# Local attention with TensorE's order written out: projections of the next head group and gates in small steps between scores, transposes and values

## The chip, the cores and the metric

The kernel runs on one core of a Trainium2 chip. A time is what the device reports for one execution, in microseconds (us). A profile is one further execution, recorded by the hardware profiler. Five engines work side by side, each through its own list of instructions in order: TensorE (PE in the profile, its weight loads PEld), VectorE (DVE), ScalarE (ACT), GpSimd (POOL) and SyncE (SP), which here only starts transfers. Semaphores hold an instruction until what it needs from another engine is done.

## The reference

One layer of an encoder on x of 1024 positions by 1024 features, with a cross-attention memory of 256 rows: RMSNorm; one input projection into attention q, k, v, a Mamba-2 branch and two gates; both branches merged by the gates; then cross-attention and an MLP. The change lies in the attention branch. There, 16 query heads of 64 features share 4 key/value heads, four to one; each block of 128 queries sees its own block of keys and those beside it (256 keys at the two edges of the sequence, 384 elsewhere):

```python
s = jnp.einsum('bnqgrd,bnkgd->bngrqk', qb, kw) * (d ** -0.5) + bias      # bias: ALiBi and the band
m = jnp.maximum(jnp.max(s, axis=-1, keepdims=True), sink_f)
p = jnp.exp(s - m)
denom = jnp.sum(p, axis=-1, keepdims=True) + jnp.exp(sink_f - m)
o = jnp.einsum('bngrqk,bnkgd->bnqgrd', p / denom, vw)
...
merged = sigmoid(gate_a) * (attn @ w_attn_branch) + sigmoid(gate_b) * (ssd @ w_ssd_branch)
```

## The kernel before

The phases follow one another: norms and transposes, the Mamba branch (`ssd`, whose TensorE order is already written by hand), attention (`attn_phase`, L584), merge and cross-attention (`merge_cross_phase`, L719), the MLP. Products are kept exact by splitting each operand into a high and a low part: `mm3` (L77) issues three matmuls per block of the inner dimension, hi·hi (L81), hi·lo (L85), lo·hi (L86). A projection of 128 features for all 1024 positions is 48 such matmuls of 512 columns, accumulated in one two-bank PSUM buffer of the pool `pg` (2 buffers). Its weights come by `wload`: a transfer started by SP into raw (2 buffers), a copy by ACT to whi (L66), a subtraction by POOL to wlo (L67).

Attention runs over four head groups kv, one key/value head with its four query heads each. Ahead of a group's blocks stand, in the program text, the K projection (kps; every second group, giving two heads kh and kl), for the first group the V projection (vp), four bias tables, and two Q projections (qps, four heads q). ACT and DVE copy each projection out of PSUM into halves that are 64 rows by 1024. Behind the blocks of a group stands one gate of ATT_GATES (gate_block, L302: a projection gps, two tanh on ACT, a store). A group has eight query blocks. For one block:

- `scores(qb)`: for each of four heads two matmuls sps (L667, L668) of 384 columns (256 at the edges), then one DVE reduction that adds the bias, writes the tile t4 (named t_… in the order) and its minimum nm (L669). On the four minima DVE then computes nm and es (L671, L672). ACT takes exp of es (L673) and of the four heads (L675), with their sums den; DVE adds and inverts den (L677, L678); POOL scales the four heads (L680).
- `values(qb)`: for each of three key blocks (two at the edges) four transposes into pt (L690), an ACT copy ph (L693) and a DVE remainder pl (L694); then two matmuls per key block into op (L699 with ph, L700 with pl). ACT copies both halves of op to oa and ob (L703, L704), POOL adds them (L705), SP stores the result to memory (d_at).

pt, sps and op share the pool `pp`, four PSUM buffers that are given out in turn. t4 has three buffers, ph and pl four, oa two, ob one. The scores of a block are issued two blocks ahead of its values.

What sets the order around the change: in `attn_phase` nothing is pinned, so a scheduler at build time orders the instructions of every engine by its own estimate of when each could start, across groups. On TensorE it thus mixes the projections of the next group and the gates between the matmuls of the blocks. The merge (L719) begins with the two END_GATES, 14 and 15, each with its first matmul kept in program order (L737, L738); then it loads the attention output back (at, 8 tiles, split by ACT at L733 and DVE at L734) and the Mamba output (yk), and multiplies them with weights into mps.

Of the kernel before, what the change touches and what calls it, by code (L numbers as in the profile page):

```python
# [11 lines left out]
ALU = mybir.AluOpType  # L12
# [17 lines left out]
ATT_GATES = ((10,), (11,), (12,), (13,))  # L30
# [553 lines left out]
def attn_phase(kx, ins, dr):  # L584
    nc, tc = kx.nc, kx.tc
    V, A, G, PE = nc.vector, nc.scalar, nc.gpsimd, nc.tensor
    with tc.tile_pool(name="p2", bufs=1) as ap:
# [30 lines left out]
        kd = {}  # L618
        for kv in range(4):
            if kv % 2 == 0:  # L620
                w = wload(kx, ins["wk"][kv // 2])
                ps = kx.pg.tile([P, S], F32, tag="g", name="kps")
                for h in range(2):
                    gemm_fm(kx, ps[:, h * 512:(h + 1) * 512], w, kx.hT[h])
# [9 lines left out]
            if kv == 0:  # L634
                v_part()
            qs, bias = [], []
            for i in range(4):
                bt = ap.tile([P, 384], F32, tag="bias", bufs=5, name="bias")
                A.activation(bt, rel, AF.Copy, scale=SLOPES[4 * kv + i])
                bias.append(bt)  # L640
            for i in range(2):
                w = wload(kx, ins["wq"][2 * kv + i])
                ps = kx.pg.tile([P, S], F32, tag="g", name="qps")
                for h in range(2):
                    gemm_fm(kx, ps[:, h * 512:(h + 1) * 512], w, kx.hT[h])
                for s in range(2):
# [4 lines left out]
                    qs.append((q, own))  # L651
            kh, kl = kd[kv]
            def scores(qb):
                kb0, kb1 = max(qb - 1, 0), min(qb + 2, NT)
                nb = kb1 - kb0
                n = nb * P
                bo = (kb0 - qb + 1) * P
                ql = slice(qb * P, (qb + 1) * P)
                keys = slice(kb0 * P, kb1 * P)
                t4 = ap.tile([P, 4, 384], F32, tag="t4", bufs=3, name="t4")  # L660
                nm = ap.tile([P, 4], F32, tag="nm", bufs=2, name="nm")
                den = ap.tile([P, 4], F32, tag="den", bufs=2, name="den")
                es = ap.tile([P, 4], F32, tag="es", bufs=2, name="es")
                for i in range(4):
                    q, own = qs[i]
                    sp_ = kx.pp.tile([P, 512], F32, tag="p", name="sps")
# [681 lines left out]
```

## Time and profile before

| | |
|---|---|
| runs shown | 2495.89 us median of 3 (2494.34 to 2497.92) |
| the profiled execution | 2500.91 us, its span 2499.1 us |
| granted clock, mean | 0.989 of full speed |
| TensorE busy | 2409.9 us, 96% |
| DVE, ACT, POOL busy | 1357.4, 1072.5, 1054.1 us |
| first score matmul to last values matmul | 1014.0 to 1292.0 us |
| four head groups, by their first score matmul | 69, 80, 70 and 59 us |

Times in the profile are microseconds from the start of the span. A row of a timeline gives start, duration, engine, line, operation, tile written <- tiles read, count, and in brackets the idle time before it with what ended it. Several equal instructions in a row are one row with their count, and the duration is then from the first start to the last end. A matmul row's duration overlaps the next one's, since TensorE works as a pipeline; the cost of a matmul is the distance to the next start.

### The profile page before, as it was taken

To read this page: it belongs to the slowest core of one execution; us is meant where nothing else is said; L and a number is where in the kernel's file an instruction comes from. 1 tells how busy PE (TensorE), PEld (TensorE's weight loads), DVE (VectorE), ACT (ScalarE), POOL (GpSimd) and SP (SyncE) were. 2 spreads that over 40 slices of the span, in tenths; PEclk is the share of its full clock that TensorE was granted. 3 is DMA by queue.
4 is the path that set the end of the run, shared out by engine and by line. 5 is a ranking of instruction groups with operands and counts; after the bars stand their busy time and mean duration, and the time that the engine had idled before them with its cause. 6 is when DMAs were issued, how large, how long until landed. Compare 5 with 4: busy or idle time off the path is not lost.

```text
span 2499.1 us, 32531 instructions
## 1 busy us (share of the span) xinstructions
PE 2409.9 (96%) x12156; PEld 1998.4 (80%) x12156; DVE 1357.4 (54%) x2048; ACT 1072.5 (43%) x2214; POOL 1054.1 (42%) x905
## 2 busy tenths in 40 slices
PE   7899999999999999999999999999999998999998
PEld 6688887878878788777778878888978876788887
DVE  5747566575665753555554352235775555454534
ACT  5436355463544544676773242235543323221211
POOL 4234526354363633444444444134685544231210
PEclk9999999999999999999999999999999998999999
DMA  6223223232322422111135453411443334442211
GB/s 224 79 66 119 68 85 109 61 122 63 103 89 74 125 64 73 43 41 47 49 120 175 148 203 121 160 68 58 136 166 114 114 127 143 173 135 85 90 62 68
DMA packets 154926, 260.47 MB, mean 104 GB/s; under 512 B 11792, under 2 KB 86672, under 8 KB 154768
## 3 DMA queue, kind: packets, MB, share of 16 engines
q1 hardware_dynamic: 83872, 219.58, 25.7%
q10 hardware_dynamic: 70896, 38.81, 5.5%
q8 instruction: 96, 1.57, 0.3%
q14 instruction: 62, 0.51, 0.1%
HBM read 210.90 MB, written 47.45 MB: 103 GB/s over the span
## 4 chain that ended last, share of the span: by engine, by line
PE 64%; DVE 13%; POOL 8%; ACT 7%; issue 6%; DMA 2%; SPq 0%; ACTq 0%; POOLq 0%; DVEq 0%
PE pb L1108 5%; PE dps L85 5%; PE dps L86 5%; PE dps L81 5%; PE mps L85 3%; PE mps L86 3%; PE mps L81 3%; PE zp L85 2%; PE zp L81 2%; PE zp L86 2%; PE pc L1108 2%; PE st L462 2%; DVE cx L350 2%; POOL prev L477 2%; POOL cb_t L476 1%
## 5 line engine op out<-in xcount | busy, mean ns | idle before, releaser
L67 POOL TENSOR_TENSOR wlo<-raw,whi 128x1024 fp32r<-128x1024 f32 x142 | 346.8, 2443 | 595.4 <-ACT whi L66 559.8
L66 ACT ACTIVATE whi<-raw 128x1024 fp32r<-128x1024 f32 x144 | 152.0, 1056 | 253.5 <-PE mps L85 115.1
L81 PE MATMUL cps<-kt,whi 128*128 128x512 f32 x512 | 217.9, 426 | 8.6 <-DVE cx L350 8.6
L86 PE MATMUL cps<-kt,wlo 128*128 128x512 f32 x512 | 201.6, 394 | 0.0
L85 PE MATMUL cps<-kt,whi 128*128 128x512 f32 x512 | 201.4, 393 | 0.0
L1074 POOL TENSOR_TENSOR wop<-w,wop 128x512 fp32r<-128x512 f32 x64 | 92.9, 1458 | 94.0 <-ACT wop L1073 94.0
L81 PEld LDWEIGHTS cps<-kt,whi 128*128 128x128 f32 x512 | 97.5, 190 | 35.0 <-issue 16.3
L85 PEld LDWEIGHTS cps<-kt,whi 128*128 128x128 f32 x512 | 97.6, 191 | 26.3 <-issue 7.3
L86 PEld LDWEIGHTS cps<-kt,wlo 128*128 128x128 f32 x512 | 97.3, 190 | 21.0
L120 POOL TENSOR_TENSOR rr<-rv,mhalf 128x1 f32<-128x1 f32 (+1 forms) x50 | 38.6, 772 | 170.1 <-DVE rv L118 167.5
L81 PE MATMUL gps<-kt,whi 128*128 128x512 f32 x256 | 108.8, 425 | 0.0
L496 ACT ACTIVATE ef<-rows,ebias 128x128 f32<-128x128 f32 x256 | 83.2, 391 | 53.3 <-PE cb L511 50.1
L680 POOL TENSOR_SCALAR t<-t,den 128x384 f32<-128x384 f32 (+1 forms) x128 | 69.1, 559 | 82.0 <-DVE den L678 62.9
L85 PE MATMUL mps<-yk,whi 128*128 128x512 f32 x256 | 100.2, 391 | 1.5 <-DVE yk L734 1.4
L86 PE MATMUL gps<-kt,wlo 128*128 128x512 f32 x256 | 101.5, 396 | 0.0
L85 PE MATMUL gps<-kt,whi 128*128 128x512 f32 x256 | 100.9, 394 | 0.0
L86 PE MATMUL mps<-yk,wlo 128*128 128x512 f32 x256 | 99.8, 390 | 0.3 <-POOL wlo L67 0.3
L81 PE MATMUL mps<-yk,whi 128*128 128x512 f32 x256 | 99.9, 390 | 0.0
L85 PE MATMUL dps<-kt 128*128 128x512 f32 x256 | 99.7, 389 | 0.0
L81 PE MATMUL dps<-kt 128*128 128x512 f32 x256 | 99.7, 389 | 0.0
L85 PE MATMUL dps<-wd,u 128*128 128x512 f32 x256 | 99.7, 389 | 0.0
L86 PE MATMUL dps<-wd,u 128*128 128x512 f32 x256 | 99.7, 389 | 0.0
(369 smaller groups left out, 7144.8 us busy)
## 6 DMA issues: line engine op xcount, KB each, us to landing
rows<-d_cs ACTq DMA_DIRECT2D x128, 256.0 KB, 3.8
raw<-in_wssd_dram SPq DMA_DIRECT2D x48, 512.0 KB, 3.3
raw<-in_wup_dram SPq DMA_DIRECT2D x40, 512.0 KB, 3.8
raw<-in_wsb_dram SPq DMA_DIRECT2D x32, 512.0 KB, 3.2
d_u<-c SPq DMA_DIRECT2D x64, 256.0 KB, 3.0
uraw<-d_u SPq DMA_DIRECT2D x32, 512.0 KB, 4.0
raw<-in_wdn_dram SPq DMA_DIRECT2D x28, 512.0 KB, 4.3
x<-in_x_dram SPq DMA_DIRECT2D x16, 512.0 KB, 7.4
```

What stands on the lines that cost most here:

```text
L66: nc.scalar.activation(hi, raw, AF.Copy)
L67: (eng or nc.gpsimd).tensor_tensor(lo, raw, hi.bitcast(F32), ALU.subtract)
L81: i = mm(out, l[0], r[0], start=first, stop=False)
L85: mm(out, l[0], r[1], start=False, stop=False)
L86: mm(out, l[1], r[0], start=False, stop=last)
L350: V.scalar_tensor_tensor(acc[:, :S - o], ps[:, o:], cw(k), acc[:, :S - o], ALU.mult, ALU.add)
L462: PE.matmul(st[:, lo:hi], q.btok[:, c], xs.rearrange("p d h q -> p (d h q)")[:, lo:hi], start=True, stop=True)
L477: G.tensor_tensor(prev[:, c - 1, 1], prev[:, c - 1, 1], t, ALU.add)
L496: A.activation(ef[:, h], rows[:, 0, h], AF.Exp, bias=kx.ebias[:, b, j, 0, o:o + 1])
L680: G.tensor_scalar(t4[:, i, :n], t4[:, i, :n], den[:, i:i + 1], 1.0, ALU.mult, ALU.mult)
L1074: self.kx.nc.gpsimd.tensor_tensor(t[:, 1], src, t[:, 0].bitcast(F32), ALU.subtract)
L1108: self.kx.nc.tensor.matmul(ps, w[:, i, ks], act[:, k, j], start=start and k == 0 and m == 0, stop=k == 3 and m == 2, skip_group_check=True)
```

## The change

Only `attn_phase` and ATT_GATES change. TensorE's order in the phase is now the order of the program text (`manual_schedule` for PE); ACT, DVE, POOL and SP are still ordered by the scheduler. The K and Q projections and the gates 10 to 13 become jobs of a `Stream`. A job is cut into 16 chunks of three matmuls, and its weights are loaded when the job ahead of it begins. The text takes each block apart into units: the three (at the edges two) sets of four transposes of the block itself (`flips`), and the four scores of the block two ahead; then the values of the block itself. `deal` spreads a given number of chunks evenly in front of these units, and the table `counts` gives the number for each of the 32 blocks. Of 14 jobs' 224 chunks 48 run ahead of the first score (as in before: a K and two Q projections with V between them), 7 in the first two scores, the rest by the table. Jobs with flag 1 are held: their matmuls run, but the copies out of PSUM are issued only with `release`, at block 5 of a group, together with the next group's bias tables. These are the last Q job of each next group and the K job of groups 2 and 3. No chunk of the END_GATES is dealt: they stay in `merge_cross_phase`.

```diff
-ATT_GATES = ((10,), (11,), (12,), (13,))
+ATT_GATES = (10, 11, 12, 13)
...
-    with tc.tile_pool(name="p2", bufs=1) as ap:
+    with tc.tile_pool(name="p2", bufs=1) as ap, tc.manual_schedule(engines={mybir.EngineType.PE}):
...
+        def k_job(kv):
+            def load():
+                return wload(kx, ins["wk"][kv // 2])
+            def run(w):
+                ps = psum_g(kx, "kps")
+                yield from fm_chunks(kx, ps, w)
...
-            t4s = {0: scores(0), 1: scores(1)}
-            for qb in range(NT):
-                if qb + 2 < NT:
-                    t4s[qb + 2] = scores(qb + 2)
-                values(qb, t4s[qb])
-            for m in ATT_GATES[kv]:
-                gate_block(kx, ins, dr, m)
+        class Stream:
...
+            def take(self, n):
+                for _ in range(n):
+                    if self.cur is None:
+                        if not self.jobs:
+                            return
+                        (_, run), hold = self.jobs.pop(0)
+                        w, self.w = self.w, self.jobs[0][0][0]() if self.jobs else None
+                        self.cur, self.left, self.hold = run(w), 16, hold
+                    next(self.cur)
+                    self.left -= 1
+                    if not self.left:
+                        if self.hold:
+                            self.held.append(self.cur)
+                        else:
+                            self.end(self.cur)
+                        self.cur = None
...
+        s = Stream([(k_job(0), 0), (q_job(0, 0), 0), (q_job(0, 1), 0), (q_job(1, 0), 0), (q_job(1, 1), 1),
+                    (gate_job(ATT_GATES[0]), 0), (q_job(2, 0), 0), (q_job(2, 1), 1), (k_job(2), 1),
+                    (gate_job(ATT_GATES[1]), 0), (q_job(3, 0), 0), (q_job(3, 1), 1)]
+                   + [(gate_job(m), 0) for m in ATT_GATES[2:]])
+        s.take(16)
+        v_part()
+        s.take(32)
+        bias_of(0)
...
+        def deal(units, n):
+            for i, unit in enumerate(units):
+                s.take((i + 1) * n // len(units) - i * n // len(units))
+                unit()
+        for b in range(2):
+            t4s[b], units = scores(0, b)
+            deal(units, 3 + b)
+        counts = ((6, 6, 6, 5, 5, 5, 2, 1), (9, 9, 9, 9, 9, 8, 3, 3), (7, 7, 7, 7, 7, 7, 3, 3),
+                  (4, 4, 3, 3, 3, 3, 3, 3))
+        for b in range(4 * NT):
+            kv, qb = divmod(b, NT)
+            pts = []
+            units = flips(qb, t4s.pop(b), pts)
+            if b + 2 < 4 * NT:
+                t4s[b + 2], more = scores((b + 2) // NT, (b + 2) % NT)
+                units += more
+            deal(units, counts[kv][qb])
+            if qb == 5 and kv < 3:
+                s.release()
+                bias_of(kv + 1)
+            values(kv, qb, pts)
+        s.take(16)
```

On TensorE, in a block of the last head group with three chunks: before had values, transposes and scores of several blocks mixed one by one, with single gate matmuls (gps) between them. Here t_11799 is block 26's tile, and the words in brackets are the engines whose semaphores the instruction waits for:

```order
L690 MATMUL pt<-ident,t_11799 128x128 [waits DVE_49,Pool_49]
L690 MATMUL pt<-ident,t_11799 128x128 [waits Pool_49] x2
L699 MATMUL op<-ph,vhl 128x512 [waits Activation_49]
L690 MATMUL pt<-ident,t_11799 128x128 [waits Pool_49]
L690 MATMUL pt<-ident,t_11799 128x128 [waits DVE_49]
L690 MATMUL pt<-ident,t_11799 128x128 x3
L85 MATMUL gps<-kt,whi 128x512
L700 MATMUL op<-pl,vhl 128x512 [waits DVE_49]
```

On this engine, in after, with t_11846 as block 27's tile, the transposes stand together, then the scores with three-matmul chunks between them, then the values:

```order
L711 MATMUL pt<-ident,t_11846 128x128 [waits DVE_49]
L711 MATMUL pt<-ident,t_11846 128x128 x3
L687 MATMUL sps<-kh,q 128x384 [waits PE_49,Activation_49]
L688 MATMUL sps<-kl,q 128x384
L81 MATMUL gps<-kt,whi 128x512
L85 MATMUL gps<-kt,whi 128x512
L86 MATMUL gps<-kt,wlo 128x512
L687 MATMUL sps<-kh,q 128x384 [waits DVE_49]
```

The first score matmul waits for ACT, which must have copied the op of the block before out of the same PSUM buffer; the next waits for DVE, which must have read a pt.

On ACT, also in the last group, before had the two copies of op ahead of the next exponentials. Here t_11799 and t_11861 are the tiles of blocks 26 and 27:

```order
L673 ACTIVATE es<-es 128x4
L675 ACTIVATE t_11799,den<-t_11799,nm 128x384 x4
L693 ACTIVATE ph<-pt 128x512 x3
L703 ACTIVATE oa<-op 64x512
L704 ACTIVATE ob<-op 64x512
L673 ACTIVATE es<-es 128x4
L675 ACTIVATE t_11861,den<-t_11861,nm 128x384 x4
```

Now, with t_11931 and t_12019 as the tiles of blocks 28 and 29:

```order
L697 ACTIVATE t_11931,den<-t_11931,nm 128x384
L695 ACTIVATE es<-es 128x4
L697 ACTIVATE t_11931,den<-t_11931,nm 128x384 x3
L729 ACTIVATE oa<-op 64x512
L730 ACTIVATE ob<-op 64x512
L714 ACTIVATE ph<-pt 128x512 x3
L729 ACTIVATE oa<-op 64x512
L695 ACTIVATE es<-es 128x4
L697 ACTIVATE t_12019,den<-t_12019,nm 128x384 x4
L730 ACTIVATE ob<-op 64x512
```

Both copies, or ob alone, now stand behind the exponentials of the block two ahead, and the copies ph of the next block behind these.

On DVE, before reduced the four scores of a block with one pl among them (block 27's tile t_11861):

```order
L694 TENSOR_TENSOR pl<-pt,ph 128x512
L669 ISA t_11861,nm<-sps,bias 128x384
L669 ISA nm 128x1
L669 ISA t_11861,nm<-sps,bias 128x384
L669 ISA nm 128x1
L669 ISA t_11861,nm<-sps,bias 128x384
L669 ISA nm 128x1
L677 TENSOR_TENSOR den<-den,es 128x4
L669 ISA t_11861,nm<-sps,bias 128x384
L669 ISA nm 128x1
L678 RECIPROCAL den<-den 128x4
L694 TENSOR_TENSOR pl<-pt,ph 128x512
```

Now the first reduction of a block (29, t_12019) stands ahead of the three pl of block 27, and its other three behind them:

```order
L699 TENSOR_TENSOR den<-den,es 128x4
L700 RECIPROCAL den<-den 128x4
L689 ISA t_12019,nm<-sps,bias 128x384
L689 ISA nm 128x1
L715 TENSOR_TENSOR pl<-pt,ph 128x512 x3
L689 ISA t_12019,nm<-sps,bias 128x384
L689 ISA nm 128x1
L689 ISA t_12019,nm<-sps,bias 128x384
```

At the end of the phase, before had 52 of the 96 matmuls of END_GATES ahead of the last values matmul and 44 behind it, ahead of the first mps; now all 96 stand behind it. The order of mps and of everything later, and of all ahead of the first score, is the same in both.

162 lines of the change are left out of this document (92 added, 70 removed).

## The prediction

> **What bounds the kernel now.** I read the page's first and fourth parts first, then the row of the attention stretch by windows, then a timeline of one block inside it.
>
> ```profile
> PE 2409.9 (96%) x12156; PEld 1998.4 (80%) x12156; DVE 1357.4 (54%) x2048; ACT 1072.5 (43%) x2214; POOL 1054.1 (42%) x905
> PE 64%; DVE 13%; POOL 8%; ACT 7%; issue 6%; DMA 2%; SPq 0%; ACTq 0%; POOLq 0%; DVEq 0%
> ```
>
> TensorE is busy for 96% of the span and carries 64% of the chain that ended last, so a change of order can only win back its waits. The change touches one stretch, from the first score matmul (1014.0) to the last values matmul (1292.0), and the seam behind it. Windows, for all instructions; the columns are the window, its length, then busy time and count of PE, PEld, DVE, ACT and POOL, the granted clock and the DMA share:
>
> ```profile
> 1014.00:1292.00 278.00, 273.85 (x1366) 213.62 (x1365) 169.69 (x490) 199.83 (x489) 137.25 (x171) 1.00 0.15 45
> 1233.00:1292.00 59.00, 57.66 (x293) 44.48 (x292) 39.18 (x120) 44.68 (x116) 31.00 (x41) 1.00 0.13 41
> ```
>
> "Busy" overstates the work there, since matmuls overlap in the pipeline; the distance between starts is what each costs. Timeline rows of PE, at places where nothing waits (start, duration):
>
> ```profile
> 1036.21 0.34 PE L667 MATMUL sps<-kh,q 128*128 128x384 f32 x1
> 1036.38 0.34 PE L668 MATMUL sps<-kl,q 128*128 128x384 f32 x1
> ...
> 1051.46 1.47 PE L690 MATMUL pt<-ident,t 128*128 128x128 f32 x12
> 1052.69 0.48 PE L86 MATMUL qps<-kt,wlo 128*128 128x512 f32 x1
> ...
> 1074.08 0.40 PE L81 MATMUL qps<-kt,whi 128*128 128x512 f32 x1
> ...
> 1082.71 0.40 PE L86 MATMUL qps<-kt,wlo 128*128 128x512 f32 x1
> 1082.94 0.28 PE L667 MATMUL sps<-kh,q 128*128 128x256 f32 x1
> 1083.06 0.28 PE L668 MATMUL sps<-kl,q 128*128 128x256 f32 x1
> ```
>
> A projection matmul costs 0.227 us (38 intervals from 1074.08 to 1082.71), a transpose 0.10 to 0.12 (twelve between 1051.46 and 1052.69 or, by their 1.47, to the last end; I take 0.11), a score matmul 0.175 over 384 keys and 0.12 over 256; a values matmul has the projection's 512 columns, so 0.227. By the code and the order of before, the stretch holds 580 projection matmuls (11 jobs of 48, and 52 of the end gates), 352 transposes, 192 and 64 score matmuls, and 176 of values: 131.7 + 38.7 + 33.6 + 7.7 + 40.0 = 251.7 us. Of the 278.0, 26.3 is waiting. That is all that a better order could win here.
>
> **The change, part by part.** First the move of the end gates. After puts all 96 matmuls behind the last values; before had 44 there. The stretch loses 52 × 0.227 = 11.8 us of work (floor 239.9) and the time behind it gains the same, which is nothing by itself. But in before the merge starved at the seam. PE and ACT rows there, and the row of the mps matmuls alone by windows (length, PE busy and count, PEld, clock):
>
> ```profile
> 1292.04 0.59 ACT L703 ACTIVATE oa<-op 64x512 f32<-64x512 f32 x1 [0.34 <-PE op L700]
> ...
> 1302.09 1.34 ACT L733 ACTIVATE at<-at 128x512 fp32r<-128x512 f32 x2 [7.89 <-DMA at<-d_at]
> ...
> 1305.90 3.23 ACT L733 ACTIVATE at<-at 128x512 fp32r<-128x512 f32 x6 [0.41 <-ACT gt L312]
> ```
> ```profile
> 1301.60 0.39 PE L86 MATMUL gps<-kt,wlo 128*128 128x512 f32 x1
> 1302.77 0.50 PE L81 MATMUL mps<-at,whi 128*128 128x512 f32 x1 [0.78 <-ACT at L733]
> ...
> 1306.58 0.50 PE L81 MATMUL mps<-at,whi 128*128 128x512 f32 x1 [1.64 <-ACT at L733]
> ...
> 1313.02 0.39 PE L81 MATMUL mps<-yk,whi 128*128 128x512 f32 x1
> ```
> ```profile
> 1301.90:1321.00 19.10, 15.90 (x58) 11.78 (x59) 0.00 (x0) 0.91 1.00 354
> ```
>
> 58 matmuls at 0.227 are 13.2 us of work in 19.1, so 5.9 us are lost. The at tiles come back from memory 10.1 us behind the last values (1302.09) and are all split by 17.1 (1309.1); 44 gate matmuls cover 10.0 us, 96 cover 21.8. Also yk, 21.0 behind in before (1313.02), would be needed only at 21.8 + 24 × 0.227 = 27.3. So the seam gives back 5.9 us. If the loads came later than in before, up to all of it would be lost again.
>
> A part of this loss is the granted clock. The windows behind the two waits:
>
> ```profile
> 1302.00:1307.00 5.00, 2.37 (x7) 1.16 (x7) 1.82 (x3) 4.39 (x8) 2.35 (x1) 1.00 1.02 341
> 1307.00:1312.00 5.00, 4.67 (x14) 3.64 (x14) 4.87 (x9) 4.06 (x9) 0.00 (x0) 0.66 1.03 392
> ```
>
> Five microseconds in which TensorE was busy for 2.37 were followed by a mean clock of 0.66. The Trainium skill ("TensorE: Matmul & The Clock Gate", "What's actually happening") lets the clock halve after an idle window of about 3.4 us; here two waits of 0.78 and 1.64 us with a few matmuls between them were enough, so a window need not be empty. By the page's rule taken literally, waits of under 3.4 us inside attention could never halve the clock, and the sum below stands; by this trace they might where they come close together, and the sum would be that of the last rival.
>
> Second, the order of the score loop. In before, one block on ACT, DVE and PE reads:
>
> ```profile
> 1033.54 0.19 ACT L673 ACTIVATE es<-es 128x4 f32<-128x4 f32 x1
> ...
> 1034.90 0.56 DVE L669 CUSTOM_DVE_ANT_0 t<-sps,bias 128x384 f32<-128x384 f32 x1 [1.16 <-PE sps L668]
> ...
> 1035.39 0.55 DVE L669 CUSTOM_DVE_ANT_0 t<-sps,bias 128x384 f32<-128x384 f32 x1
> ...
> 1036.15 0.60 ACT L693 ACTIVATE ph<-pt 128x512 fp32r<-128x512 f32 x1
> ...
> 1036.76 0.56 DVE L669 CUSTOM_DVE_ANT_0 t<-sps,bias 128x384 f32<-128x384 f32 x1
> ...
> 1037.33 0.66 DVE L694 TENSOR_TENSOR pl<-pt,ph 128x512 fp32r<-128x512 f32 x1
> ...
> 1037.61 2.26 POOL L680 TENSOR_SCALAR t<-t,den 128x384 f32<-128x384 f32 x4 [2.62 <-PE pt L690]
> ...
> 1037.91 0.30 DVE L671 TENSOR_TENSOR nm<-nm,snk 128x4 f32<-128x4 f32 x1
> ...
> 1038.69 1.28 DVE L694 TENSOR_TENSOR pl<-pt,ph 128x512 fp32r<-128x512 f32 x2
> 1038.83 0.59 ACT L703 ACTIVATE oa<-op 64x512 f32<-64x512 f32 x1
> ...
> 1039.44 0.59 ACT L704 ACTIVATE ob<-op 64x512 f32<-64x512 f32 x1
> ...
> 1039.93 0.19 ACT L673 ACTIVATE es<-es 128x4 f32<-128x4 f32 x1
> ```
>
> One block lasts 6.4 us there (es to es), and the DVE reductions of the next scores run while ACT takes the exponentials. In after they can't, in many blocks: pt, sps and op take four PSUM buffers in turn, eight per block, so the first sps of a block gets the buffer of the op before it, and the order shows its matmul waiting for ACT, which copies that op (oa, ob) only behind the four exponentials. DVE then reduces this first score ahead of the three pl, and the other scores behind them. The pieces close into a ring, from one block's exponentials to the next's: es and exponentials 2.61 (1033.54 to 1036.15), oa and ob 1.20, score matmul to reduction 0.55 (1036.21 to 1036.76), first reduction 0.57, three pl 1.86 (0.66 the first, 1.28 two), three reductions 1.54, nm 0.30, about 0.1 of handing over: 8.7 us. POOL's 2.26 lies beside it. With 256-wide scores it is about 7.8, with two pl 8.1 (an estimate: 0.23 less per score, 0.6 per pl).
>
> TensorE's own work in a full block is 12 × 0.11 + 8 × 0.175 + 6 × 0.227 = 4.09 us and 0.68 per dealt chunk: 8.2 with six chunks, 7.5 with five, 6.1 with three, and 8.9 or 10.2 with seven or nine, where it covers the ring. So what waits remain, from the table of counts:
> - first group: 0.5 in two blocks, 1.2 in three, then the block of two chunks (work 5.0 against 7.8) 2.8 and of one (3.9 against 8.1) 4.2: 11.7;
> - second: its two blocks of three chunks (5.7 against 7.8, 5.2 against 8.1) 5.0, and two kh copies of the held K job, 2.0, standing ahead of an oa: 7.0;
> - third: the same two blocks without K: 5.0;
> - fourth: one block of four chunks 1.9, four of three chunks 2.6 each: 12.2;
> - entry and end of the stretch, where softmax of the first and last block has nothing beside it: 4, an estimate from den to pl of a block, with the bounds 2 and 8;
> - six blocks have oa ahead of the exponentials instead: ACT then waits out the six values matmuls (1.36 and the copy) and the ring is 0.7 longer: 4.2.
> Together 44.1 against 26.3. The stretch becomes 239.9 + 44.1 = 284.0, +6.0; the gates behind it +11.8; the seam −5.9: **+11.9 us**, 2512.8 beside the profiled execution's 2500.9. The median of the runs shown is 5.0 below that execution, so I forecast 2507.8, **2508**.
>
> The other edits cost nothing that I can find: each job's weights are still fetched one job ahead (a job is 16 chunks, over 10 us), and merging, MLP and all ahead of the stretch keep their order. In short the time is 32.2 us below the waits W: W − 32.2 is the difference. No change asks for W = 32, before's own 26.3 would make 5.9 faster.
>
> **The rivals.**
> *TensorE stays the bound (faster).* The ring needs ob behind the exponentials and DVE's first reduction ahead of pl. If blocks run at before's 6.4, only K's 2.0, the ends' 4 and few losses in one- to three-chunk blocks remain (about 4): W = 10, −22, 2474. It decides from a ring under 7.6. For it: the dealing takes out the waits for values and transposes that before has, and the 59.0 us of the last group show that blocks could run at 7.4 with projections. Against: engines execute in order, and these orders are written into the program. 0.25.
> *A shorter ring (no change).* If hand-overs overlap more than my sum, as PEld's early loads do, a ring of 7.8 to 8.3 gives W of 27 to 37, within 0.2% (5 us, about what a measurement of this kernel can tell from no change): 2491 to 2501. 0.16.
> *The clock halves (slower still).* In the ring's three-chunk blocks TensorE works 6.1 of 8.7 us, with several short waits close together. If they halved the clock, as behind 1302 to 1307, the 6.1 would be 12.2, 3.5 over the ring in some nine blocks: +31 on top, 2539. The Trainium skill (same page, "A second HAM failure mode: psum-queue depth-cycling") describes a kernel that lost its clock by cycling PSUM buffers. No row of before does: its 26.3 us of waits went with a clock of 1.00. 0.06.
> That the order isn't what the code says is excluded by the order itself.
>
> **How the numbers follow.** The forecast has 0.53, its own range 2501 to 2520: ring 8.4 to 9.0 moves W by ±5, the ends by −2 to +4, the seam by up to +6. The range of 2483 to 2522 takes in no change and the milder half of the faster case; left out are the rest of it (0.14) and the halved clock (0.06). Faster by over 0.2%: 0.25; within: 0.16; slower: 0.53 + 0.06 = 0.59.
>
> **What would show it.** In the profile of after: es to es about 8.7 in the last group's three-chunk blocks, with an oa/ob pair behind the exponentials; PE waits put down to ACT ob or DVE at sps; the last group no shorter than the 59.0 us of before although 11.8 us of gates have left it; mps without waits for at, and a clock of 1.00 at the seam. Wrong is the prediction if es to es there is below 7.6, or if the stretch from the first score to the last values is under 272 us.

## The result, and the profile after

The changed kernel takes 2523.93 us, the median of four runs (2520.30 to 2533.61), against 2496.38 for the kernel before (2494.34 to 2497.92): a ratio of 1.0111 with a 95% interval of 1.0081 to 1.0141, about 27.5 us slower. Forecast were 2508 and a range of 2483 to 2522, so the time lies 2 us above the range. The sign was right, the size was not: the sum gave 11.9 us.

The profiled execution of after took 2521.76 us, its span 2520.0. The page's first and fourth parts:

```profile
PE 2405.2 (95%) x12156; PEld 2004.4 (80%) x12156; DVE 1351.7 (54%) x2048; ACT 1072.1 (43%) x2214; POOL 1053.1 (42%) x905
PE 61%; DVE 12%; POOL 9%; ACT 8%; issue 6%; DMA 3%; ACTq 0%; SPq 0%; POOLq 0%; DVEq 0%
```

The engines do the same work; TensorE's share of the chain fell from 64% to 61%, ACT's and POOL's rose. Where the time lies is read by comparing the starts of the same matmuls in the two profiles; the end of the last op is taken as its start and the 0.23 us that a values matmul costs:

| stretch | before | after | difference | forecast |
|---|---|---|---|---|
| first vp to first sps | 44.8 | 48.4 | +3.6 (the first vp is 0.3 earlier) | 0 |
| first sps to end of last op | 277.9 | 296.9 | +19.0 | +6.0 |
| last op to first mps, and first to last mps | 11.0 + 271.3 | 23.5 + 265.5 | +6.7 | +5.9 |
| all behind | | | −8.1 | 0 |

The last row is code that is the same in both. In it before had the granted clock down more often; two windows of 160 us, 29 us apart as the two programs are there (the third number from the end is the clock). Of before, then of after:

```profile
2011.00:2171.00 160.00, 144.69 (x585) 115.19 (x585) 83.32 (x110) 47.83 (x73) 61.91 (x39) 0.94 0.47 163
```
```profile
2040.00:2200.00 160.00, 145.89 (x621) 116.89 (x620) 86.80 (x113) 47.86 (x73) 60.84 (x39) 0.99 0.48 163
```

I take that for chance of one execution: from the last mps on, the profiles of the fourteen experiments below, where this code is the same too, took 916.3 to 921.4 us, after 916.6 and before 924.7. Up to the end of the merge after is 29.0 us behind, about what the medians say (27.5). So the change costs 3.2 ahead of the stretch, 19.0 in it, 6.7 behind it.

The stretch in after by windows (all of it, then the last head group, columns as in the prediction):

```profile
1017.10:1314.00 296.90, 265.15 (x1313) 214.06 (x1313) 166.91 (x490) 198.91 (x487) 136.75 (x171) 0.96 0.14 41
```
```profile
1235.75:1313.95 78.20, 65.89 (x307) 51.61 (x308) 39.07 (x123) 49.22 (x125) 36.99 (x45) 0.91 0.15 45
```

With a floor of 239.9 the waits W are 57.0, where the sum had 44.1. The last group takes 78.2 us, against 59.0 in before although it has 11.8 us less to do. Its granted clock is 0.91; in before it was 1.00.

A turn, here and below, is the time from the first score matmul of one block to that of the next; blocks are counted through all groups, 0 to 31. One turn of the forecast ring in after, in the first head group, rows of ACT, DVE and PE from one timeline (start, duration, and in brackets the wait and what ended it):

```profile
1055.55 0.59 ACT L730 ACTIVATE ob<-op 64x512 f32<-64x512 f32 x1
...
1056.17 1.58 ACT L714 ACTIVATE ph<-pt 128x512 fp32r<-128x512 f32 x3
1056.20 0.44 PE L687 MATMUL sps<-kh,q 128*128 128x384 f32 x1 [0.56 <-ACT ob L730]
...
1056.85 0.56 DVE L689 CUSTOM_DVE_ANT_0 t<-sps,bias 128x384 f32<-128x384 f32 x1 [1.33 <-PE sps L688]
...
1057.34 1.88 DVE L715 TENSOR_TENSOR pl<-pt,ph 128x512 fp32r<-128x512 f32 x3
...
1059.13 0.55 DVE L689 CUSTOM_DVE_ANT_0 t<-sps,bias 128x384 f32<-128x384 f32 x1
...
1060.82 0.16 DVE L693 TENSOR_TENSOR nm<-nm,snk 128x4 f32<-128x4 f32 x1
...
1061.08 0.62 ACT L697 ACTIVATE t<-t,nm 128x384 f32<-128x384 f32 x1 [3.33 <-DVE nm L693]
...
1063.58 0.57 ACT L729 ACTIVATE oa<-op 64x512 f32<-64x512 f32 x1
...
1064.18 0.59 ACT L730 ACTIVATE ob<-op 64x512 f32<-64x512 f32 x1
...
1064.83 0.44 PE L687 MATMUL sps<-kh,q 128*128 128x384 f32 x1 [0.55 <-ACT ob L730]
```

Read it from top to bottom: ob ends, the score matmul starts at once, DVE reduces it, makes three pl, reduces the other three scores, nm; ACT waits 3.33 us for this nm, then takes exponentials, oa and ob; ob ends and the next score matmul starts. 8.63 us from 1056.20 to 1064.83; 8.7 was forecast. The four turns of this kind in the first group are 8.3, 8.6, 8.5 and 8.6. The waits of the whole stretch name the link (PE's, then the weight loads' ahead of the same matmuls; total, times, longest):

```profile
PE sps L687 <- ACT ob L730: 17.4, 13, 3.2
```
```profile
PEld sps L687 <- ACT ob L730: 21.3, 13, 3.5
```

In before ACT ob held sps for 2.3 us in all, at the weight loads. At the seam TensorE waits for no at tile in after, as forecast; mps takes 265.5 instead of 271.3. The clock of 1.00 that the prediction asked for there came late, and the gates behind the last values took 23.5 us where 21.8 were in the sum:

```profile
1314.30:1317.60 3.30, 3.30 (x10) 2.52 (x9) 0.00 (x0) 1.18 (x2) 1.27 (x1) 0.50 0.44 159
1317.70:1337.50 19.80, 19.80 (x88) 16.41 (x88) 10.07 (x13) 11.76 (x20) 2.41 (x1) 1.00 0.87 280
```

### The profile page after: what moved, and what is told of

The parts are those of the page before. It is cut to its first block, busy times and chain, and to the rows that moved or that the text cites. A ratio compares the mean times of both kernels' runs of the same rounds, so it can differ in the third digit from the quotient of the medians.

```text
span 2520.0 us, 32567 instructions
## 1 busy us (share of the span) xinstructions
PE 2405.2 (95%) x12156; PEld 2004.4 (80%) x12156; DVE 1351.7 (54%) x2048; ACT 1072.1 (43%) x2214; POOL 1053.1 (42%) x905
## 4 chain that ended last, share of the span: by engine, by line
PE 61%; DVE 12%; POOL 9%; ACT 8%; issue 6%; DMA 3%; ACTq 0%; SPq 0%; POOLq 0%; DVEq 0%
PE pb L1202 5%; PE dps L85 5%; PE dps L81 5%; PE dps L86 5%; PE mps L86 3%; PE mps L85 3%; PE mps L81 3%; PE zp L85 2%; PE zp L81 2%; PE zp L86 2%; PE pc L1202 2%; PE st L462 2%; POOL wlo L67 2%; ACT t L697 2%; DVE cx L350 2%
## 5 line engine op out<-in xcount | busy, mean ns | idle before, releaser
L81 PE MATMUL gps<-kt,whi 128*128 128x512 f32 x256 | 113.8, 445 | 2.1 <-DVE q L651 2.1
L85 PE MATMUL gps<-kt,whi 128*128 128x512 f32 x256 | 102.9, 402 | 0.0
L85 PE MATMUL dps<-kt 128*128 128x512 f32 x256 | 99.7, 390 | 0.0
L86 PE MATMUL dps<-wd,u 128*128 128x512 f32 x256 | 99.7, 389 | 0.0
L81 PE MATMUL dps<-kt 128*128 128x512 f32 x256 | 99.7, 389 | 0.0
L86 PE MATMUL dps<-kt 128*128 128x512 f32 x256 | 99.7, 389 | 0.0
```

What stands on the lines that cost most here:

```text
L81: i = mm(out, l[0], r[0], start=first, stop=False)
L85: mm(out, l[0], r[1], start=False, stop=False)
L86: mm(out, l[1], r[0], start=False, stop=last)
```

## Experiments

Each is the changed kernel with one edit, unless said otherwise. Ratios are to the kernel before on the same chip; after has 1.0111. "The stretch" is from the first sps to the end of the last op in the run's profile, 296.9 in after. It comes from one execution: experiment 6, with the same order of every engine in it, has 299.8, so a difference of up to 3 us in it is not read as an effect by itself. Single turns repeat better, 29 of the 31 within 0.3 us.

**1. A link of the ring made longer: ob copied twice.**

```diff
             A.activation(ob, op[64:128], AF.Copy)
+            A.activation(ob, op[64:128], AF.Copy)
```

> The changed kernel with ACT's copy of op to ob done twice, one behind the other (0.60 us more of ACT per block, 32 blocks; no other work). Ring theory (the first score of a block waits for ob, behind the exponentials): the 18 or so blocks that the ring sets grow by 0.6 each, so about +11 us, 2535 against 2524, and TensorE's wait of sps for ACT ob grows from 38.7 to about 49. Rival, TensorE's own written order or DVE sets the pace: ACT is busy for 199 of 297 us and takes the copy beside other work, 0 to 3 us.

Measured: 1.0177 (1.0157 to 1.0197), about 16 us over after; the stretch 316.0, +19.1. The waits of the stretch:

```profile
PE sps L687 <- ACT ob L731: 37.2, 21, 3.8
```
```profile
PEld sps L687 <- ACT ob L731: 44.5, 21, 4.2
```

The matmuls' waits for ob went from 17.4 in 13 places to 37.2 in 21; with the weight loads', which the expectation counted in, from 38.7 to 81.7. ACT was idle for almost a third of the stretch, and still the added copies lengthen it by about as much as all 32 of them take (19 us): ob is on the path. It is not 0.6 in every block: the first head group grew by 8.7 us and the second by about 1. The 19.1 are more than the 11 expected, since some blocks with seven and nine chunks became longer than their work too, and the clock fell from 0.96 to 0.95.

**2. TensorE work that is not in the ring: transposes of the last group issued twice.**

```diff
-                for i in range(4):
+                for i in list(range(4)) * rep:
                     PE.transpose(pt[:, i * P:(i + 1) * P], t4[:, i, kb * P:(kb + 1) * P], kx.ident)
...
-            units = flips(qb, t4s.pop(b), pts)
+            units = flips(qb, t4s.pop(b), pts, 2 if b >= 24 else 1)
```

> The changed kernel with each transpose of the last head group issued twice in a row (88 more transposes of about 0.11, 9.7 us of TensorE work, about 1.3 a block, the same result). Ring theory with the halved clock on top: TensorE has 2.6 us of slack in each of these blocks, the work hides, and less idling keeps the clock up, so the last group (78.1 us from its first score's block, 1235.9, to the last values, 1314.0) gets shorter by up to 10 and its clock returns to about 1.00: 2514 to 2522. Ring theory without a part of the clock: within 2 us. Rival, TensorE's own work sets the pace there: +10, 2534.

Measured: 1.0111 (1.0090 to 1.0133), no change. The last group by windows:

```profile
1237.30:1313.80 76.50, 70.47 (x395) 57.59 (x395) 38.89 (x123) 49.48 (x125) 37.01 (x45) 0.98 0.15 46
```

88 more transposes, 9.7 us of work, and the group is 1.7 us shorter (76.5 for 78.2), with the clock at 0.98 for 0.91. Four turns that took 9.9, 10.3, 11.0 and 8.8 us take 8.6, 10.0, 8.8 and 8.8. Behind the last scores, where no ring turns, the group is 1.3 longer. So TensorE's work does not set the pace in these turns, and the 3.8 us that they lost went with the return of the clock.

**3. The slack filled with real work: end gates dealt into the last group.**

```diff
-                   + [(gate_job(m), 0) for m in ATT_GATES[2:]])
+                   + [(gate_job(m), 0) for m in ATT_GATES[2:] + END_GATES])
...
-                  (4, 4, 3, 3, 3, 3, 3, 3))
+                  (6, 5, 5, 5, 5, 5, 5, 6))
...
-        for m in END_GATES:
-            gate_block(kx, ins, dr, m, pin=True)
```

> The changed kernel with the two end gates dealt as well: the last group gets 42 chunks in place of 26 (5 or 6 a block), 16 chunks stay behind the last values, near the 44 matmuls of before. Ring theory: a block's work is 7.5 to 8.2 us against a ring of 8.7, so the added 10.9 us of work hide, the clock stays at 1.00 in the last group, which gets no longer than its 78.1 us and by the clock up to 10 shorter; the gates behind the last values fall from 23.5 to 11; the seam loses 5 to 6 again. Together -6 to -16: 2508 to 2518. Rival, TensorE's work sets the pace: the gates only move and the seam is lost, +6: 2530.

Measured: 1.0121 (1.0098 to 1.0145), not the 6 to 16 us of gain. The last group took 84.7, not 78 or less. Its turns of the ring hardly changed (61.9 us from its first score to its last block's, 61.4 in after) although 5 chunks stand where 3 did. But two things were left out of the expectation. Behind the last scores no ring turns: there the added chunks are simply added (22.8 us for 16.8). And a gate brings its own copies into the ring, two tanh (1.1), a whi (1.06) and a wlo. Four turns of the group by windows (length, then PE, PEld, DVE, ACT, POOL, clock):

```profile
1259.30:1269.20 9.90, 8.10 (x41) 6.48 (x41) 5.71 (x15) 7.25 (x18) 5.91 (x7) 1.00 0.36 119
1269.20:1279.30 10.10, 9.67 (x41) 7.71 (x41) 4.63 (x15) 5.22 (x15) 3.44 (x6) 0.83 0.06 15
1279.30:1287.90 8.60, 8.09 (x41) 6.47 (x41) 4.55 (x15) 5.27 (x15) 3.36 (x5) 1.00 0.06 15
1287.90:1298.90 11.00, 8.10 (x41) 6.47 (x41) 6.75 (x15) 7.32 (x18) 6.14 (x7) 0.98 0.33 109
```

Where ACT has 18 operations instead of 15 the turn takes 9.9 and 11.0 at a clock of 1.00 and 0.98; the plain turn takes 8.6, and the same with a clock of 0.83 takes 10.1.

**4. Another place for the values: one later.**

```diff
             units = flips(qb, t4s.pop(b), pts)
+            if b:
+                units.append(lambda a=last: values(*a))
+            last = (kv, qb, pts)
...
-            values(kv, qb, pts)
+        values(*last)
         s.take(16)
```

> The changed kernel with each block's values put one place later on TensorE: transposes of a block, then values of the block before, then the scores two ahead. The op buffer is then no longer the one that the next first score waits for, and ACT can take ph ahead of the next exponentials. Ring theory: the block falls from 8.7 to about 6.6 where few chunks are dealt, the stretch from 296.9 us to 260 to 272, so -25 to -37: 2487 to 2499, about the kernel before. Rival, the dealing in a fixed order itself costs the time, wherever values stand: within 8 us of 2524.

Measured: 1.0037 (1.0023 to 1.0052), 18.5 us faster than after; the stretch 279.2. The first waits of the list:

```profile
PE sps L687 <- DVE pl L715: 6.6, 4, 3.4
PE gps L81 <- DVE q L651: 3.5, 1, 3.5
```

One wait of 1.7 us for ob is left, where after had 13 with 17.4 us, and the turns of the last group are 6.0 to 8.8, 7.3 in the mean. The gain is less than the 25 to 37 expected: 13.7 us still go from score to score at the release of Q and K, and the turns with a gate's copies stay at 8 to 9. Most of the 27.5 us is thus not the price of a written order as such, but of this one.

**5. The same TensorE order, ACT's copies ahead of the exponentials.** The exponentials of scores are issued behind the values of the block two earlier, and each is kept behind the instruction ahead of it.

```diff
-                A.activation(es, es, AF.Exp)
-                for m in range(4):
-                    A.activation(t4[:, m, :n], t4[:, m, :n], AF.Exp, ...)
+            def soft(pin=True):
+                keep = tc.keep_in_program_order if pin else (lambda i: i)
+                keep(A.activation(es, es, AF.Exp))
+                for m in range(4):
+                    keep(A.activation(t4[:, m, :n], t4[:, m, :n], AF.Exp, ...))
...
             values(kv, qb, pts)
+            if b + 2 < 4 * NT:
+                soft()
```

> The changed kernel with ACT's exponentials of a block pinned behind oa and ob of the block two earlier; TensorE's order as in the change. Ring theory: ACT then waits for the values matmuls instead. The ring becomes oa and ob 1.20, es and exponentials 2.61, first ph and three pl 2.4, last score 0.35, six values matmuls with their landing 1.56: about 8.1 instead of 8.7, so the stretch gets 5 to 14 us shorter than 296.9, and 2510 to 2520 in all. If the place of the two copies alone made the ring, blocks would fall to before's 6.4 and the stretch by 30. Rival, TensorE or DVE sets the pace: within 3 us.

Measured: 1.0072 (1.0054 to 1.0089), about 10 us faster than after; the stretch 285.3, −11.6, inside the 5 to 14. sps no longer waits for ob but, less, for DVE:

```profile
PE sps L687 <- DVE nm L689: 7.3, 12, 1.2
```

Five of the last group's seven turns fell to 7.0 to 7.6 (the first and the last took 9.4 and 9.6), its clock was 1.00 from 1240 to 1300. The two turns at the release took 21.9, as in after (22.1). TensorE's order in the stretch is the same, matmul for matmul, as in after; ACT's new order, with what the scheduler made of it on DVE and POOL, is worth 10 us, and not the 30 that it would be if the place of the two copies were the whole of it.

**6. V's weights ahead of the first Q job's.**

```diff
+        vw = [wload(kx, ins["wv"][kh]) for kh in range(2)]
         s.take(16)
-        v_part()
+        v_part(vw)
```

> The changed kernel with V's weights loaded ahead of the first Q job's, as in before (in the change the stream fetches the next job's weights first). If V's late weights cost the 3.2 us between the first vp and the last, the first score comes 3.2 earlier behind the first vp and the whole is 2 to 4 us shorter: 2521. If the difference there was chance, no change.

Measured: 1.0095 (1.0077 to 1.0114). In after the V projection waits once:

```profile
PE vp L85 <- POOL wlo L67: 1.8, 1, 1.8
```

Here it doesn't, and the first sps comes 44.8 us behind the first vp as in before (48.4 in after). The stretch is 299.8 in this profile, 2.9 more than in after, mostly by the end of the last group (80.6 for 78.2), where every engine's order is the same: executions can differ by that much there. So the 3.2 us ahead of the stretch are shown by the profile, and the ratio agrees within its interval without proving it. Experiment 5 parts the wait from the clock: its V weights are as late as in after (the same wait of 1.8), but its clock stays at 1.00 from 970 to 990, where after has 0.91, and the first sps comes 46.9 behind the first vp.

**7. K's copies parted:** those for group 2's head at the end of the job, those for group 3's head at block 15.

```diff
-                yield from fm_chunks(kx, ps, w)
-                for s in range(2):
+                def out(s):
...
+                for n, _ in enumerate(fm_chunks(kx, ps, w)):
+                    if n == 15:
+                        out(0)
+                    yield
+                out(1)
...
+            if qb == 7 and kv == 1:
+                s.release(2)
```

> The changed kernel with the copies of the held K projection parted: those of group 2's head at the end of the job, those of group 3's head two blocks later than now. Ring theory with the projections' copies on it: blocks 15 and 16 (12.5 and 9.6 us from score to score) lose the four kh copies that stand ahead of oa and ph, 4.1 us, and part of the idling that halves the clock there (0.68 in 1157 to 1167): the two fall to 16 to 18 together, 4 to 6 us less, 2519. Rival, Q and the gates' PSUM wait for DVE q make these blocks long: under 2 us.

Measured: 1.0113 (1.0097 to 1.0130). The two turns of blocks 15 and 16 took 13.7 and 7.0, 20.7 for 22.1: mostly the rival. TensorE's longest wait there is now one of 5.38 us of the first gate matmul for DVE's q, since both PSUM buffers for projections are held until Q and K are copied out.

**8. All of it together:** 4, 6 and 7, the end gates dealt with 20 chunks left behind the last values, and counts of ((6,6,6,6,6,6,7,7),(7,6,6,6,7,7,6,6),(6,6,6,6,6,6,4,4),(5,5,5,5,4,4,4,4)).

> All that the runs pointed to so far in one kernel: values one place later as in the run before (ring about 6.6 to 8), V's weights first, K's copies parted, the two end gates dealt as well with 20 chunks left behind the last values, and 4 to 7 chunks in every block. Ring theory: a block's work is 6.8 to 8.9 us, at or over the ring nearly everywhere, so waits in the stretch fall to 12 to 25 from 57, the gates behind still cover the loads of at, and the clock stays up: 2470 to 2488, faster than before by 0.3 to 1%. If a written order costs time in itself, it stays above 2500.

Measured: 1.0057 (1.0042 to 1.0072), 2513.8, a clear miss and slower than 4 alone. Its stretch is 289.8 with 12 chunks (8.2 us) more in it, and the waits are few and long:

```profile
PE sps L691 <- DVE pl L719: 14.7, 7, 4.2
PE gps L81 <- DVE q L655: 7.2, 1, 7.2
```

Many turns take what their work takes (8.3 with six chunks), but one took 17.1, at the release, and one 12.2.

**9. The low parts of the weights on DVE instead of POOL,** by `wload(..., eng=V)` in the three kinds of job. Why: small DVE operations in after last ten times their usual 0.16 us while POOL makes a wlo. DVE's row and POOL's:

```profile
1271.65 1.99 DVE L693 TENSOR_TENSOR nm<-nm,snk 128x4 f32<-128x4 f32 x1
```
```profile
1271.23 2.38 POOL L67 TENSOR_TENSOR wlo<-raw,whi 128x1024 fp32r<-128x1024 f32 x1 [1.02 <-ACT whi L66]
```

> The changed kernel with the low parts of the weights of its 14 projection jobs taken by DVE instead of POOL (about 1.2 us each on DVE, 2.4 less on POOL). In the trace of the change four small DVE operations (nm, es) last 0.8 to 2.3 us instead of 0.16 and end with a wlo of POOL. If POOL's wlo holds them up, these disappear (6.9 us of excess in small DVE operations falls under 2), the four blocks get shorter by about 1 to 2 each, and the stretch falls by 2 to 5 from 296.9 although DVE has 15 us more to do. If DVE's in-order work is what counts, the stretch grows by 5 to 15.

Measured: 1.0085 (1.0069 to 1.0100); the stretch 295.6, −1.3 where 2 to 5 were expected. Two of the four long operations are gone; the excess, the time over 0.16 us of those that last above 0.6, is 4.0 us for 6.9, not under 2. The turn of 12.5 is 11.1 and that of 10.0 is 9.2, but the one behind the release is 10.4 for 9.6 and the last group is longer (80.7). The direction is as expected; neither the stretch nor the ratio is clear of noise.

**10 and 11. Version 8 with the K job ahead of the last Q job of group 2 and 24 chunks left behind (the second row of counts then ends in 5,7, the fourth is 5,4,4,4,4,4,4,3); and the same with the low parts on DVE.**

```diff
-                    ..., (q_job(2, 0), 0), (q_job(2, 1), 1), (k_job(2), 2),
+                    ..., (q_job(2, 0), 0), (k_job(2), 2), (q_job(2, 1), 1),
```

> As the run with values later and everything dealt, with the K job ahead of the last Q job of group 2 (its copies no longer meet that Q job's at the release) and 24 chunks left behind the last values instead of 20. Ring theory with the projections' copies on it: the block of 17.1 us falls to about 10, the seam's 5 us come back, so 8 to 12 us less than that run's 2514: 2502 to 2506, within 0.4% of before. If it is the held PSUM buffer alone that makes that block long, 2510 to 2514.

> The run beside it with the low parts of the weights taken by DVE. If POOL's wlo holds up DVE's small operations in it (13.1 us of excess in the earlier version), 3 to 8 us less than the run beside it, 2495 to 2501, about the kernel before; if DVE's in-order work counts more, 5 to 10 more.

Measured: 1.0040 (1.0027 to 1.0053) and 1.0016 (1.0005 to 1.0026). The stretches:

```profile
1015.50:1297.70 282.20, 260.15 (x1338) 216.30 (x1337) 171.53 (x490) 198.38 (x487) 135.67 (x170) 0.98 0.15 44
```
```profile
1017.40:1292.20 274.80, 258.54 (x1338) 213.28 (x1337) 179.59 (x501) 198.56 (x487) 111.60 (x159) 0.99 0.15 45
```

The texts of the pair differ in the engine of wlo alone: 7.4 us of the stretch, excess in small DVE operations 2.7 for 7.5, waits of sps for DVE pl 5.4 for 12.3. Two turns make up 7.1 of it, 7.8 for 12.2 and 7.8 for 10.5. In both the nm of version 10 lasts 2.1 to 2.4 us beside a wlo, with a wait of TensorE behind it; in the first:

```profile
1101.21 2.37 DVE L697 TENSOR_TENSOR nm<-nm,snk 128x4 f32<-128x4 f32 x1
...
1109.09 0.69 PE L691 MATMUL sps<-kh,q 128*128 128x384 f32 x1 [4.18 <-DVE pl L719]
```

But the scheduler also moved copies: in version 11 a ph stands ahead of the exponentials in both turns, in version 10 all three stand behind them. So the hold on DVE is on the path here, by up to 2 us a time; what of the 7.4 is the hold's and what the other order's, the pair does not part. The block at the release still took 16.0 and 15.5, not 10, with 5.8 us of it in the gate's wait for DVE q: the expectation of 10 failed on the held PSUM buffer, its own rival.

**12. Version 11 with bias tables on POOL and the end gates whole behind the last values,** counts ((6,6,6,6,6,6,7,7),(7,6,6,6,7,7,3,7),(6,6,6,7,7,6,4,4),(3,3,3,3,3,3,3,3)).

> The last version (values later, V's weights first, K's copies parted and early, low parts of the weights on DVE) with the bias tables made by POOL instead of ACT (16 of about 0.52 us off ACT), the end gates left whole behind the last values as in the change, and three chunks in each block of the last group. Ring theory: with values later the last group's ring is 6.3 to 8, so fewer chunks there cost up to 3 us of waits against 6.1 of work, 7.4 x 8; the 5 us lost at the merge come back since 32 chunks cover its loads; the release at block 13 has 2 us less on ACT. 5 to 10 us less than that version (1.0016 of before): 0.994 to 0.999 of before, 2485 to 2498. If not, waits behind the release and in the last group stay as they are, 1.000 to 1.003.

Measured: 1.0004 (0.9992 to 1.0015): the kernel before, to a measurement. Against version 11 that is some 3 us, not 5 to 10, and the intervals overlap. The stretch is 276.9, and from there to the last mps it takes 21.9 + 265.8 = 287.7, for 294.4 in version 11, although 8 more chunks stand in it.

**13. Experiment 2 in all blocks that wait most** (`2 if b >= 22 or 14 <= b < 18 else 1`).

> The changed kernel with each transpose issued twice in a row in the blocks that wait most (14 to 17 and 22 to 31: 148 more transposes, about 16 us of TensorE work, the same result). If the halved clock lengthens these blocks, which is 0.88 to 0.91 there in the change, the clock returns to 0.97 or more and the stretch gets shorter than 296.9 by 2 to 6 despite the work: the part of the miss that is the clock's. If clock and added work balance, within 2 us. If the clock costs nothing there because ACT and DVE set the ring, the stretch grows by up to 5, where blocks come near TensorE's bound.

Measured: 1.0127 (1.0109 to 1.0146); the stretch 297.4, +0.5. The last group and, before it, the blocks at the release, by windows:

```profile
1150.00:1179.00 29.00, 23.15 (x126) 19.30 (x125) 20.86 (x48) 20.89 (x47) 10.77 (x14) 0.94 0.11 33
1241.00:1315.00 74.00, 67.67 (x390) 54.99 (x389) 36.73 (x114) 47.07 (x121) 34.71 (x44) 1.00 0.15 46
```

16 us of added work hide, the clock from 1241 on is 1.00; the group is 77.0 for 78.2, with the same four turns as in experiment 2 (8.6, 10.0, 8.8, 8.8), but three turns behind the release are 3 us longer. The stretch is the same within 2 us, the second outcome: clock and added work balance.

**14. Version 12 with no chunk in block 14,** second and third rows of counts (7,6,6,6,7,7,0,8),(6,6,7,7,7,7,4,4).

> The last version with no chunk in block 14, where the first gate matmul waited 5.8 us for a PSUM buffer that Q's copies hold behind the release, and those three chunks dealt later. If that wait stood on the path, blocks 14 and 15 (14.4 and 7.4 us from score to score) fall to 18 or 19 together and the whole by 2 to 4 us, 0.9985 to 0.9995 of before; if the ring of the two blocks is what lasts (7 to 8 each with Q's and K's copies on ACT), under 1 us.

Measured: 1.0009 (0.9999 to 1.0020). The gate's wait is gone and the two turns take 19.4 for 21.8, between the two expectations, but the third group gave 2.3 of it back (72.7 for 70.4), and the whole is no shorter. No version ran faster than before.

## Why the prediction was right in sign and wrong in size

**The ring: right.** The turn was sized to 0.1 to 0.4 us where it runs alone (8.3 to 8.6 for 8.7; its three pl, put at 1.86 beside rows that add up to 1.94, took 1.88 in the turn above). That ob closes it is shown from both sides: made longer, it lengthens the stretch by 19.1 (1); moved, TensorE's waits for ob fall from 17.4 to 1.7 (4) or to none (5). **The floor: nearly.** Blocks that TensorE bounds took 0.2 to 1.1 more than their work (below).

**The seam: right.** +6.7 for +5.9. The waits for at went, as forecast; the gates were 1.7 over the sum's 21.8, which is what 3.4 us of halved clock cost; in experiment 12, as in the sum, they took 21.9.

**The step that failed first: "merging, MLP and all ahead of the stretch keep their order".** True of TensorE, and I looked no further. The stream fetches a job's weights when the job ahead begins, so the first Q job's raw, whi and wlo stand ahead of V's on SP, ACT and POOL. 3.2 us: 1.8 of wait and, behind it, 3.4 us of halved clock (0.50 from 973.0 to 976.3), which cost half their length; experiment 5, with the wait and without the halving, came 1.5 earlier.

**The step that failed most: the waits of the stretch,** 44.1 in the sum, 57.0 measured. Three terms of it:

- *The release.* Priced were two turns and two kh copies, 17.9. From block 15's scores to block 17's it took 22.1. All copies that the release issues stand in ACT's and DVE's queues at once: the two kh ahead of oa, but also q, bias and a whi, and TensorE waits for both q and ob. DVE's es, too, lasted 2.28 us there instead of 0.16, until a wlo of POOL ended, and ACT waited 1.45 us for it. Together 4.2 us more; experiment 7 parted the kh copies and won 1.4. ACT, PE and window rows of after (the third number from the end is the clock):

```profile
1157.19 0.20 ACT L695 ACTIVATE es<-es 128x4 f32<-128x4 f32 x1 [1.45 <-DVE es L694]
...
1158.47 0.50 PE L81 MATMUL gps<-kt,whi 128*128 128x512 f32 x1 [2.13 <-DVE q L651]
...
1162.72 0.58 PE L687 MATMUL sps<-kh,q 128*128 128x256 f32 x1 [2.85 <-ACT ob L730]
```
```profile
1157.00:1167.00 10.00, 5.01 (x18) 3.92 (x19) 6.62 (x12) 9.41 (x19) 3.25 (x6) 0.68 0.21 66
```

- *The clock.* The sum took 1.00, and gave the halved clock to a rival with a chance of 0.06 and a price of 31. It came in part: 0.96 over the stretch, 0.91 in the last group. Experiments 2 and 13 show its share there, 3.8 us over four turns. It is less than 31 because the clock came back each time: the two halvings inside these turns lasted 3.4 us (1259.7 to 1263.0) and 6.8 (1276.7 to 1283.5), where the rival had every such block halved throughout.
- *The other copies on the ring.* I priced projections by their matmuls, and what comes with them at nothing. Each job also puts a whi and two q copies or tanh on ACT and a wlo on POOL, and wlo held up DVE's nm by 1.8 us in the turn at 1267 (10.3 us at a clock of 0.97). In experiment 3 the turns with a gate's copies were 1.3 to 2.4 longer than the plain one.

Five turns of the last group that I put at 8.7, and three of them 0.7 longer for oa, 45.6 together, took 48.0: the last two points, 2.4. With the release's 4.2 that is 6.6 of the 12.9. About 4 more are blocks that I had at no loss, since TensorE bounds them (10.4 to 10.6 for 10.2 in the second group, 9.2 to 10.0 for 8.9 in the third); the rest, some 2, I could not put to a place. Neither was tested, and their cause stays open.

**The rivals.** "TensorE stays the bound" fell with the first row of waits: the ring turns in 8.6 where TensorE's work is shorter than that. That blocks could run at 6.4 to 7.4 was about right (6.0 to 8.8 in experiment 4, mostly 7.0 to 7.6 in 5), but it takes another place for the values or another order on ACT. "A shorter ring" fell too. The range ended at 2522 because each unknown was allowed to add only to its own term; none covered a queue that I hadn't followed, nor a clock halved in part.

## What to carry to other kernels

When one engine's order is written out by hand, follow the ring that closes through the others: what frees the PSUM buffer of the next first instruction, and what stands ahead of that on its engine. Price a moved projection by its copies and weight splits as well as by its matmuls, and follow every load that a new order puts ahead of another. A stretch with slack for TensorE is not always free: here stretches of 3.4 us in which it was about half idle were sometimes followed by a halved clock.

## What the runs showed of the hardware

**The clock can halve behind 3.4 us of half work, and need not.** After by windows of 1 us (the first number behind the length is TensorE's busy time, the third from the end the clock):

```profile
1256.00:1257.00 1.00, 0.41 (x2) 0.00 (x0) 0.23 (x2) 0.98 (x4) 0.00 (x0) 1.00 0.00 0
1257.00:1258.00 1.00, 0.61 (x2) 0.30 (x2) 0.16 (x2) 0.97 (x3) 0.70 (x2) 1.00 0.00 0
1258.00:1259.00 1.00, 0.43 (x2) 0.43 (x3) 1.00 (x3) 0.85 (x2) 1.00 (x3) 1.00 0.00 0
1260.00:1261.00 1.00, 1.00 (x4) 0.90 (x4) 1.00 (x4) 0.00 (x0) 0.82 (x1) 0.50 0.00 0
1262.00:1263.00 1.00, 1.00 (x4) 0.90 (x4) 0.44 (x1) 0.00 (x0) 0.00 (x0) 0.50 0.56 131
```

TensorE was busy for 0.41, 0.61 and 0.43 of three microseconds, with no single wait above 0.9 us, and from about 1259.7 to 1263 the granted clock was 0.50. The share alone does not decide it. Of the next three windows the first was followed by the halving, the other two, about as idle, by a clock of 1.00 (from 1290.4 to 1293.8 and from 1297.2 to 1300.6):

```profile
1256.25:1259.65 3.40, 1.86 (x8) 1.29 (x8) 2.04 (x7) 2.55 (x6) 2.35 (x5) 1.00 0.00 0
1287.00:1290.40 3.40, 1.89 (x8) 1.17 (x8) 1.66 (x6) 2.93 (x8) 1.64 (x3) 1.00 0.01 2
1293.80:1297.20 3.40, 1.65 (x12) 1.23 (x10) 0.34 (x2) 3.35 (x12) 0.00 (x0) 1.00 0.11 24
```

The first group's turns of 8.3 to 8.6 us with 7.5 us or more of work, and experiment 5's of 7.0 to 7.6 with 6.1, kept 1.00. The Trainium skill ("TensorE: Matmul & The Clock Gate", "What's actually happening") speaks of an idle window of about 3.4 us: the length agrees with the 3.4 us of halved clock here, but an idle window was not needed.

**POOL holds up small DVE operations.** An nm of 0.16 us took 1.99 and ended at 1273.64, 0.03 behind POOL's wlo; an es took 2.28 and ended at 1157.16, 0.02 behind another. It is not new with after: in before the 32 es took 0.52 us in the median and 1.13 at most, and one of them, for example, ended at 1032.55, 0.01 behind one of POOL's scalings of t. The Trainium skill ("SBUF — State Buffer", "Who interferes with whom") calls this an exclusive lock on a port pair that the two engines share; the traces agree. Experiment 11, with that POOL work moved to DVE, took 7.4 us out of a stretch of 282, but the order of copies changed with it, so the price of the hold alone is not shown.
